# Down projection pairs one slot further behind the units whose rows they use

## The chip, the cores and the metric

The kernel runs on one core of one Trainium2 chip. The metric is the device time of one execution in microseconds, as the median of several runs. A core has five engines with instruction lists of their own, which meet through semaphores: TensorE (PE in the profile, its weight loads PEld), VectorE (DVE), ScalarE (ACT), GpSimd (POOL) and SyncE (SP), which here issues the loads of weights. TensorE writes its sums to PSUM, which has eight banks of 128 x 512 values; VectorE and ScalarE read them from there.

## The reference

Two layers over 256 positions of width 2048. Layer one mixes with a gated short convolution, layer two with latent attention; after each stands an MLP with squared ReLU, and after each part a layer norm of the scaled residual plus the part. The change lies in the MLPs alone:

```
def sq_relu_mlp(x, w1, w2):
    return jnp.square(jax.nn.relu(x @ w1)) @ w2

h = layer_norm(ALPHA * h + sq_relu_mlp(h, mlp_w1[layer], mlp_w2[layer]),
               ln_g[layer, 1], ln_b[layer, 1])
```

`w1` is 2048 x 8192 and `w2` 8192 x 2048, all in float32.

## The kernel before

**Numbers.** Every float32 operand is split in a high and a low part of TensorE's own format: `split` (lines 134 to 137) makes the high part with a copy on ScalarE and the low part with a subtraction on VectorE. A product then takes three terms: high by high, high by low, low by high. Weights arrive as `raw` tiles of 128 x 1024 in a ring of 7, and their parts `hi` and `lo` lie in rings of 9. `take` (line 192) hands out the next weights of the stream and prepares those that come after, up to a fixed distance ahead.

**Passes, units, slots.** The 8192 hidden columns are worked in 8 passes q of 8 units m. A *unit* makes 128 hidden columns for 256 positions: 16 steps of two matmuls, a high one of 512 columns (line 224) and a low one of 256 (line 228), into one PSUM bank. `whole` (line 363) adds the two halves of the bank: ScalarE copies one to SBUF (line 366), VectorE adds (line 367) into the tile `fp`, which holds two units; there is one buffer for `fp`. ReLU and square follow on ScalarE (line 732) once both units are there; the last two units of a pass of the fast kind are treated singly ("late"), the second on VectorE (line 728).

Pass 0 and pass 7 use the plain down projection (`down`). Passes 1 to 6 use a scheme with seven products instead of eight for 2 x 2 blocks. For each two units, `finish_pair` (line 650) makes sums of row blocks on VectorE (`form`, lines 645 to 648) and splits the 896 columns into *rows* `factors` (`h1c`, `h1a` in layer one, `h3c`, `h3a` in layer two; c holds rows 0 and 1, a rows 2 and 3). A *pair* (p, i) of the down projection, `products_of` and `fast_products`, multiplies the rows of units 2j and 2j+1 of pass p, j = i mod 4, with seven combinations of weight blocks: 21 matmuls of 512 columns (lines 309, 311, 312), in seven PSUM banks. Its weights (`w2f`) need more work than those of a unit: one combination on VectorE at line 171, two of half size at lines 175 and 178, and four splits (lines 136, 137). Pairs 0 to 3 serve one half of the output columns, pairs 4 to 7 the other, with the same four rows. Behind pair 3, ScalarE copies the seven banks out (line 620) and the other half's in (line 693), a burst of 14 copies. After pass 6, `fold` adds the products together, eight additions for each half (line 628).

**Order.** `steps` (line 89) gives the order of units and pairs. A *slot* is a unit and, behind it, a pair:

```
for q in range(1, NQ):
    for m in range(QC):
        p, i = (q, m - SHIFT) if m >= SHIFT else (q - 1, m + QC - SHIFT)
        yield q, m, (p, i // NB, i % NB, (p % 2) ^ (i // NB)) if p in FAST else None
```

(There, the second entry is the half and the third is j; with i as used here, pair (p, i) stands SHIFT slots behind unit (p, i).) With SHIFT = 5, pair (1,0) stands in slot (1,5), pair (1,3) in slot (2,0), pair (1,4) in slot (2,1). Units (1,0) to (1,4) and (7,5) to (7,7) have no pair: they are *lone*. A lone unit of even m uses the bank of product 6, the others the bank "unit". The rows of a pass overwrite those of the pass before, and the old rows 0 are last read by pair 4, in slot m = 1: so `finish_pair(0, u)` is called behind that slot's pair, and the other rows at m = 3, 5 and 7 as soon as their two units are done.

The written order is not quite the order on the engines: when the program is made, each engine's list is ordered by which instructions could go, and an instruction whose buffer is still taken lets later ones pass.

`mm_run` (line 230) makes a unit; at step 2 (`TURNED`) of units for which `TURN` is true the low matmul stands before the high one. In layer two (`extra`) the transposed residual is added to the sums behind units 0 to 3 of pass 1. At the end of layer one the residual is read back from memory (line 763, `xback`) into the place that the folded sums leave, and at the end of layer two `last_sum` copies the sums to PSUM, where the plain down projection goes on.

Of the kernel before, what the change touches and what calls it, by code (L numbers as in the profile page):

```python
# [18 lines left out]
T = 256  # L19
D = 2048  # L20
NC = D // P
FF = 4 * D
NQ = 8
QC = FF // NQ // P
# [10 lines left out]
NB = 4  # L35
BW = D // NB
FAST = range(1, NQ - 1)
SHIFT = 5


def TURN(q, m, extra):
    return m == 0 or not (q == 1 and m < SHIFT or q == NQ - 1 and m > SHIFT) or extra and q == 1 and m <= NB
FIRST = (0, 1, 2, 3, 4, 6, 8, 12, 16)
LEAD = 4
HEAD = 4
# [2 lines left out]
TURNED = 2  # L48
# [8 lines left out]
def trunk(ctx: ExitStack, tc: tile.TileContext, xT, vecs, lead, w_first, w_in, w_out, w_kv, w_q, w_uk, w_uv,  # L57
# [31 lines left out]
    def steps():  # L89
# [5 lines that stand above are left out]
# [15 lines left out]
    class Banks:  # L110
# [15 lines left out]
        @classmethod  # L126
        def next(cls):
            cls.count += 1
            return (cls.count - 1) % (4 if cls.more is None else 8)
# [4 lines left out]
    def split(hi, lo, src):  # L134

        nc.scalar.copy(hi, src)  # L136
        nc.vector.tensor_tensor(lo, src, hi.bitcast(F32), ALU.subtract)  # L137
# [54 lines left out]
    def take(halves=2, look=LOOK):  # L192

        i = state["next"]
        state["next"] += halves
        ahead = -sum(size(j) for j in range(i, i + halves))
        for j in range(i, len(stream)):
            for step in range(size(j)):
                ahead += 1
                if ahead > look:  # L200
                    return [ready.pop(i + k) for k in range(halves)]
                if j < 2 * HEAD:
                    continue
                steps = begun.setdefault(j, [prepare(j), 0])
                if steps[1] == step:
                    next(steps[0])
                    steps[1] += 1
        return [ready.pop(i + k) for k in range(halves)]

    def psum(name, bank=None):  # L210

        bank = Banks.next() if bank is None else bank
        return (pmm if bank < 4 else Banks.more).tile([P, 512], F32, tag=f"mm{bank}", name=name)
# [8 lines left out]
    def high(ps, w, blk, x, first):  # L222

        nc.tensor.matmul(ps, w[blk // 8][0][:, blk % 8, :], x, start=first, stop=False)  # L224

    def low(ps, w, blk, x, last):

        nc.tensor.matmul(ps[:, :T], w[blk // 8][1][:, blk % 8, :], x[:, :T], start=False, stop=last)  # L228

    def mm_run(wps, x, k0, k1, nk, turned=None):  # L230

        for k, (w, ps) in [(k, u) for k in range(k0, k1) for u in wps]:
            if k == turned:
                low(ps, w, k, x[k], False)
            high(ps, w, k, x[k], k == 0)
            if k != turned:
                low(ps, w, k, x[k], k == nk - 1)
# [125 lines left out]
    def whole(ps, out):  # L363

        t = tmp.tile([P, T], F32, tag="evac", name="t")
        nc.scalar.copy(t, ps[:, T:])  # L366
        nc.vector.tensor_tensor(out, ps[:, :T], t, ALU.add)  # L367
# [157 lines left out]
    xhl = [t[:, k, :] for t in xts for k in range(NC // 2)]  # L525
# [17 lines left out]
    for k0, k1 in pieces:  # L543
        half, at = k0 // 8, slice(k0 % 8, (k1 - 1) % 8 + 1)
        xt = xts[half][:, at, :]
        x, w = sources[k0]
# [12 lines left out]
    for m in range(NC):  # L559
        part = []  # L560
        for what in "cub":
            ps = next(pss)
            f = cbuf[:, m % 2, "cub".index(what), :T]
# [22 lines left out]
    def mlp(idx, ln, blocks, fast, begin=None, extra=None, last=False):  # L586
# [5 lines left out]
        xhl = [xt[:, k, :] for k in range(NC)]  # L592
# [40 lines left out]
        def last_sum(n, t, bank):  # L633

            finals[n, t] = psum("ps_e", bank)
            nc.scalar.copy(finals[n, t], block(n, t))
# [4 lines left out]
        def form(u):  # L641

            a21, a11, a12, s1, s2, s4 = (u[:, i * P:(i + 1) * P] for i in (0, 1, 3, 4, 6, 7))
            two = u.rearrange("p (i c) -> p i c", c=P)
            nc.vector.tensor_tensor(s1, a21, u[:, 2 * P:3 * P], ALU.add)
            nc.vector.tensor_tensor(two[:, 5:7, :], two[:, 0:5:4, :], a11.unsqueeze(1).to_broadcast([P, 2, P]),
                                    ALU.subtract)
            nc.vector.tensor_tensor(s4, a12, s2, ALU.subtract)

        def finish_pair(j, u):  # L650
            f = factors[j // 2][:, j % 2]
            if q in FAST:
                form(u)
                split(f[:, 0, :], f[:, 1, :], u[:, P:])
            else:
                split(f[:, 0, :2 * T], f[:, 1, :2 * T], u[:, :2 * T])

        q = 0
        for m in range(QC):
# [11 lines left out]
            f = tmp.tile([P, T], F32, tag="fh", name="fh", bufs=3)  # L671
# [10 lines left out]
        factors = [act.tile([P, QC // 4, 2, 7 * P], F32R, tag=tag, name=f"h{idx}{tag}") for tag in ("c", "a2")]  # L682
# [3 lines left out]
        def resume(p, g, at=None):  # L686

            ps[p] = psum(f"ps_{p}", bank[at or p])
            onto.discard(p)
            if p in OWN and begun[g] == FAST[0]:  # L690
                fresh.add(p)
            else:
                nc.scalar.copy(ps[p], place(p, g))
                onto.add(p)

        begun = {0: FAST[0], 1: FAST[0]}

        def products_of(p, i, j, g):

            nonlocal folds  # L700
            order = [f[0] for f in FACTORS]
            end = i == 0 or p == FAST[-1]
            fast_products(ps, factors, j, set(fresh), order if j == NB - 1 and end else (), onto)
            fresh.clear()
            if j == NB - 1 and end:
                begun[g] = 0
                for o in order:
                    put_back(o, g, ps[o])
                    if i == 0:
                        resume(o, 1 - g)  # L710
            if p == FAST[-1] and j == NB - 1:
                folds = chain(folds, fold(g))

        for q, m, pair in steps():
            lone = pair is None
            if q == FAST[0] and m == SHIFT:
                for o, _, _ in FACTORS:
                    resume(o, 1)
            w = take(2, 7)
            at = "6" if lone and m % 2 == 0 else "unit"  # L720
            un = psum("ps_u", bank[at])
            mm_run([(w, un)], xhl, 0, NC, NC, turned=TURNED if TURN(q, m, extra) else None)
            if m % 2 == 0:
                u = fast.tile([P, 8 * P], F32, tag="fp", name="fp")
            whole(un, u[:, (m % 2) * T:(m % 2 + 1) * T])
            late = q in FAST and m >= QC - 2
            if late and m % 2:
                nc.vector.scalar_tensor_tensor(u[:, T:2 * T], u[:, T:2 * T], 0.0, u[:, T:2 * T], ALU.max, ALU.mult)
            elif late or m % 2:
                for function in (AF.Relu, AF.Square):  # L730
                    at = u[:, :T] if late else u[:, :2 * T]
                    nc.scalar.activation(at, at, function)  # L732
            if m % 2 and (m > 1 or lone):
                finish_pair(m // 2, u)
            if extra and q == FAST[0] and m < NB:
                for t in range(2):
                    extra(block, m, t, spare[1 + (2 * m + t) % 3])
            if begin and q == FAST[0] and m < 4:
                if m % 2 == 0:
                    nc.gpsimd.dma_start(parked[:, 4 * m:4 * m + 8, :], held_x[0][:, 4 * m:4 * m + 8, :])  # L740
            if q == FAST[0] and m == SHIFT:
                sums = act.tile([P, 4, 2, BW], F32, tag="xres", name=f"sums{idx}")
            if q == NQ - 1:
                for _ in range(3 if m >= SHIFT else 2):
                    next(folds, None)
            if pair:
                products_of(*pair)
            if m == 1 and not lone:
                finish_pair(0, u)
            if q == NQ - 1 and last and m >= QC - 2:  # L750
                for t in range(2):
                    last_sum(m - QC + 2, t, spare[2 * (m - QC + 2) + t])
# [41 lines left out]
    with tc.tile_pool(name="fast1", bufs=1) as fast:  # L794
        mlp(1, before, to_wide, fast, begin=prepare_chunks)


    with tc.tile_pool(name="att", bufs=1) as ap:
# [64 lines left out]
        f = tmp.tile([P, T], F32, tag="fh", name="fpe", bufs=3)  # L863
# [223 lines left out]
    with tc.tile_pool(name="fast2", bufs=1) as fast:  # L1087
        mlp(3, after, to_out, fast, extra=turn_residual, last=True)
# [95 lines left out]
```

## Time and profile before

| | |
|---|---|
| median of 3 runs | 2000.79 us (1999.85 to 2004.03) |
| profiled execution | 2002.59 us, of it span 2000.7 us |
| granted clock of TensorE, mean | 0.998 |
| busy TensorE, VectorE, ScalarE | 1988.5, 1720.3, 1289.0 us |
| read from memory | 383.87 MB, 194 GB/s over the span |
| units and pairs, layer one | from 452.78 to 1001.80 us |
| units and pairs, layer two | from 1400.35 to 1947.56 us |

The profile shows one execution. Busy time of an engine is counted per instruction; "idle before" names what ended an idle stretch. A row of a timeline has start, duration, engine, line of the kernel, operation, what it writes and from what it reads, with shapes, and in brackets the idle time before it and what released it. The duration of a matmul includes its way through the array; the distance of the starts of two is what it costs in a stream.

### The profile page before, as it was taken

The numbers are of one execution on the slowest core, as the hardware profiler recorded it, in microseconds if no ns is written. First come the engines' busy times: TensorE is split into PE (matmuls) and PEld (weight loads), VectorE is DVE, ScalarE is ACT, GpSimd is POOL, SyncE is SP. The second block draws the span as 40 slices with busy tenths as digits, with TensorE's granted clock in tenths as the row PEclk, the third lists the DMA queues.
The fourth block names the chain that finished last, engine by engine and source line by source line (L and its number), as shares of the span: only waits on it lengthen the run. The fifth ranks groups of instructions, "written<-read, shape, count | busy, mean of one in ns | idle before, by whom it ended". The sixth has DMA issues, their size and how long they took to land.

```text
span 2000.7 us, 29698 instructions
## 1 busy us (share of the span) xinstructions
PE 1988.5 (99%) x11062; PEld 1732.5 (87%) x11062; DVE 1720.3 (86%) x2505; ACT 1289.0 (64%) x1914; POOL 5.6 (0%) x27
## 2 busy tenths in 40 slices
PE   9999999999999999999999999999999999999998
PEld 8888888988788888888889998898888888888886
DVE  8667667787899999999988988778889999999995
ACT  6444445586667777677756665558666776767772
POOL 0000000000000000000000000000000000000000
PEclk9999999999999999999999999999999999999999
DMA  9766666574565555665764643656456556565572
GB/s 339 213 190 189 189 189 190 182 238 143 180 215 191 200 194 196 210 205 204 246 223 153 184 144 106 211 182 196 140 194 216 170 203 216 180 212 197 205 267 96
DMA packets 107712, 390.00 MB, mean 195 GB/s; under 512 B 11952, under 2 KB 12720, under 8 KB 107056
## 3 DMA queue, kind: packets, MB, share of 16 engines
q1 hardware_dynamic: 106560, 383.79, 58.7%
q0 software_dynamic: 864, 4.19, 0.6%
q8 instruction: 86, 1.41, 0.3%
q14 instruction: 58, 0.48, 0.1%
q10 hardware_dynamic: 144, 0.13, 0.0%
HBM read 383.87 MB, written 4.19 MB: 194 GB/s over the span
## 4 chain that ended last, share of the span: by engine, by line
PE 95%; DMA 2%; DVE 1%; issue 1%; ACT 0%; SPq 0%; DVEq 0%; POOLq 0%; ACTq 0%
PE ps_u L224 20%; PE ps_l L224 13%; PE ps_u L228 10%; PE ps L312 7%; PE ps L311 7%; PE ps L309 7%; PE ps_l L228 7%; PE ps_d L312 2%; PE ps_d L309 2%; PE ps_d L311 2%; PE ps_w L258 2%; PE ps_w L257 2%; PE ps_w L256 2%; DMA raw<-in_w2f_dram 1%; PE ps_g L258 1%; PE ps_g L256 1%
## 5 line engine op out<-in xcount | busy, mean ns | idle before, releaser
L137 DVE TENSOR_TENSOR lo<-raw,hi 128x1024 fp32r<-128x1024 f32 x710 | 854.6, 1218 | 167.1 <-ACT hi L136 97.6
L136 ACT CAST hi<-raw 128x1024 fp32r<-128x1024 f32 x710 | 732.5, 1054 | 220.2 <-PE ps_l L224 102.2
L224 PE MATMUL ps_u<-xhl,hi 128*128 128x512 f32 x1792 | 621.2, 393 | 0.0
L228 PE MATMUL ps_u<-xhl,lo 128*128 128x256 f32 x1792 | 485.0, 280 | 0.0
L224 PEld LDWEIGHTS ps_u<-xhl,hi 128*128 128x128 f32 x1792 | 328.8, 187 | 67.5 <-DVE fp L367 0.9
L228 PEld LDWEIGHTS ps_u<-xhl,lo 128*128 128x128 f32 x1792 | 338.1, 189 | 12.9
L224 PE MATMUL ps_l<-xhl_a,hi 128*128 128x512 f32 x704 | 244.1, 393 | 0.0
L228 PE MATMUL ps_l<-xhl_a,lo 128*128 128x256 f32 x704 | 195.4, 279 | 0.0
L136 ACT CAST hi_t<-raw_t 128x1024 fp32r<-128x1024 f32 x96 | 101.5, 1057 | 120.4 <-DVE raw_t L171 115.4
L224 PEld LDWEIGHTS ps_l<-xhl_a,hi 128*128 128x128 f32 x704 | 132.1, 188 | 29.9
L228 PEld LDWEIGHTS ps_l<-xhl_a,lo 128*128 128x128 f32 x704 | 131.9, 188 | 0.2
L171 DVE TENSOR_TENSOR raw_t<-raw,raw 128x1024 f32<-128x1024 f32 x96 | 116.9, 1217 | 9.8 <-DMA raw<-in_w2f_dram 9.8
L137 DVE TENSOR_TENSOR lo_t<-raw_t,hi_t 128x1024 fp32r<-128x1024 f32 x96 | 116.9, 1218 | 2.1 <-ACT hi_t L136 1.7
L366 ACT COPY t<-ps_u 128x256 f32<-128x256 f32 x112 | 41.7, 372 | 95.0 <-PE ps_u L228 94.7
L224 PE MATMUL ps_l<-z,hi 128*128 128x512 f32 x240 | 82.4, 391 | 0.0
L258 PE MATMUL ps_w<-xd,hi 128*128 128x258 f32 x256 | 72.7, 284 | 0.0
L256 PE MATMUL ps_w<-xd,hi 128*128 128x258 f32 x256 | 72.3, 282 | 0.0
L257 PE MATMUL ps_w<-xd,lo 128*128 128x258 f32 x256 | 72.3, 282 | 0.0
L224 PE MATMUL ps_l<-oT,hi 128*128 128x512 f32 x208 | 71.3, 391 | 0.0
L732 ACT ACTIVATE fp<-fp 128x512 f32<-128x512 f32 (+1 forms) x112 | 65.9, 588 | 7.2 <-DVE fp L367 6.8
L178 DVE TENSOR_TENSOR raw<-raw 128x512 f32<-128x512 f32 x96 | 66.1, 688 | 2.0
L175 DVE TENSOR_TENSOR raw<-raw,raw_t 128x512 f32<-128x512 f32 x96 | 65.6, 683 | 0.8
(350 smaller groups left out, 3880.0 us busy)
## 6 DMA issues: line engine op xcount, KB each, us to landing
raw<-in_w_dram SPq DMA_DIRECT2D x320, 512.0 KB, 4.1
raw<-in_w2f_dram SPq DMA_DIRECT2D x192, 512.0 KB, 5.2
raw<-in_w_in_dram SPq DMA_DIRECT2D x88, 512.0 KB, 3.7
raw<-in_w_out_dram SPq DMA_DIRECT2D x32, 512.0 KB, 3.7
raw<-in_w_o_dram SPq DMA_DIRECT2D x32, 512.0 KB, 4.2
raw<-in_w_kv_dram SPq DMA_DIRECT2D x10, 512.0 KB, 4.6
raw<-in_w_q_dram SPq DMA_DIRECT2D x8, 512.0 KB, 4.0
raw<-in_w_uk_dram SPq DMA_DIRECT2D x8, 512.0 KB, 4.6
```

The source lines that it names most:

```text
L136: nc.scalar.copy(hi, src)
L137: nc.vector.tensor_tensor(lo, src, hi.bitcast(F32), ALU.subtract)
L171: nc.vector.tensor_tensor(t.rearrange(two, a=2), b12.unsqueeze(1).to_broadcast([P, 2, BW]), r1.rearrange(two, a=2), ALU.subtract)
L178: nc.vector.tensor_tensor(t4, b21, b12, ALU.subtract)
L224: nc.tensor.matmul(ps, w[blk // 8][0][:, blk % 8, :], x, start=first, stop=False)
L228: nc.tensor.matmul(ps[:, :T], w[blk // 8][1][:, blk % 8, :], x[:, :T], start=False, stop=last)
L256: nc.tensor.matmul(ps[:, :W], hi, x[k][:, :W], start=k == 0, stop=False)
L257: nc.tensor.matmul(ps[:, :W], lo, x[k][:, :W], start=False, stop=False)
L258: nc.tensor.matmul(ps[:, :W], hi, x[k][:, W:], start=False, stop=k == NC - 1)
L309: nc.tensor.matmul(ps, x[0], w[0], start=first, stop=False, skip_group_check=onto)
L311: nc.tensor.matmul(ps[:, at], x[0], w[1][:, at], start=False, stop=False, skip_group_check=onto)
L312: nc.tensor.matmul(ps, x[1], w[0], start=False, stop=last, skip_group_check=onto)
```

## The change

SHIFT goes from 5 to 6. Pair (q, i) now stands six slots behind unit (q, i): pair (1,0) in slot (1,6), pair (1,3) in slot (2,1), pair (1,4) in slot (2,2), pair (1,5) in slot (2,3). Lone units are now (1,0) to (1,5) and (7,6), (7,7). Old rows 0 and 1 are read until slots m = 2 and 3, so the new rows 0 and 1 are finished behind the pairs of those slots; a table `rows` keeps their `fp` tile until then. The parts of units 6 and 7 of pass 7 are squared and split one by one, like the late units of the other passes, instead of as two together. The bank of a lone unit goes by the distance to SHIFT, and `TURN` no longer asks whether the residual is added in (`extra`).

```
-SHIFT = 5
-def TURN(q, m, extra):
-    return m == 0 or not (q == 1 and m < SHIFT or q == NQ - 1 and m > SHIFT) or extra and q == 1 and m <= NB
+SHIFT = 6
+def TURN(q, m):
+    return m == 0 or not (q == 1 and m < SHIFT or q == NQ - 1 and m > SHIFT)
...
+        rows = {}
...
-            at = "6" if lone and m % 2 == 0 else "unit"
+            at = "6" if lone and (m - SHIFT) % 2 else "unit"
             un = psum("ps_u", bank[at])
-            mm_run([(w, un)], xhl, 0, NC, NC, turned=TURNED if TURN(q, m, extra) else None)
+            mm_run([(w, un)], xhl, 0, NC, NC, turned=TURNED if TURN(q, m) else None)
             if m % 2 == 0:
                 u = fast.tile([P, 8 * P], F32, tag="fp", name="fp")
             whole(un, u[:, (m % 2) * T:(m % 2 + 1) * T])
-            late = q in FAST and m >= QC - 2
+            late = m >= QC - 2
...
-            if m % 2 and (m > 1 or lone):
-                finish_pair(m // 2, u)
+            if late and q not in FAST:
+                f, at = factors[m // 4][:, 1], slice(m % 2 * T, (m % 2 + 1) * T)
+                split(f[:, 0, at], f[:, 1, at], u[:, at])
+            else:
+                rows[m // 2] = u
+            if m % 2 and (m > 3 or lone) and m // 2 in rows:
+                finish_pair(m // 2, rows.pop(m // 2))
...
             if pair:
                 products_of(*pair)
-            if m == 1 and not lone:
-                finish_pair(0, u)
+            if m in (2, 3) and not lone:
+                finish_pair(m - 2, rows.pop(m - 2))
```

## The prediction

> **What bounds the kernel now.** I read the page first (span, chain, busy engines), then the waits of TensorE, then the time of single units and pairs in windows, and last the timelines around the few waits.
>
> ```profile
> span 2000.7 us, 29698 instructions
> PE 1988.5 (99%) x11062; PEld 1732.5 (87%) x11062; DVE 1720.3 (86%) x2505; ACT 1289.0 (64%) x1914; POOL 5.6 (0%) x27
> PE 95%; DMA 2%; DVE 1%; issue 1%; ACT 0%; SPq 0%; DVEq 0%; POOLq 0%; ACTq 0%
> ```
>
> TensorE is busy for 99% of the span and holds 95% of the chain. The change leaves its work as it is: the same 112 units and 96 pairs. So a gain can come only from TensorE's waits, and these are short:
>
> ```profile
> PE ps L312 <- DVE h1a L137: 2.2, 1, 2.2
> PE ps_d L312 <- DVE h1a L137: 1.2, 1, 1.2
> PE ps L312 <- DVE h3a L137: 1.1, 1, 1.1
> PE ps L309 <- ACT h1a L136: 0.7, 1, 0.7
> ```
>
> All four (engine and line, what it waited for: total, times, longest) are for rows `h1a` or `h3a`, the factors made from units 4 to 7. The windows below give what each cost. Columns: stretch, its length, busy time of PE, PEld, DVE, ACT and POOL with counts, granted clock, DMA share, GB/s. Edges are the first matmuls of the unit or pair and of the one after it.
>
> ```profile
> 458.34:463.89 5.55, 5.55 (x34) 4.89 (x33) 3.04 (x4) 2.38 (x3) 0.00 (x0) 1.00 0.84 266
> 501.57:507.14 5.57, 5.57 (x34) 4.89 (x33) 4.35 (x5) 2.75 (x4) 0.00 (x0) 1.00 0.86 274
> 507.14:511.94 4.80, 4.80 (x23) 3.85 (x22) 4.04 (x6) 3.91 (x5) 0.00 (x0) 1.00 0.06 17
> 511.94:518.48 6.54, 5.81 (x33) 4.80 (x32) 6.07 (x9) 1.55 (x3) 0.00 (x0) 1.00 0.87 308
> 518.48:528.53 10.05, 7.87 (x22) 5.91 (x23) 6.03 (x7) 6.67 (x11) 0.00 (x0) 0.66 0.45 147
> 650.00:900.00 250.00, 250.00 (x1278) 212.77 (x1277) 238.48 (x290) 179.73 (x246) 0.00 (x0) 1.00 0.59 200
> 953.94:955.30 1.36, 1.36 (x7) 1.00 (x6) 1.36 (x3) 1.36 (x3) 0.00 (x0) 1.00 0.79 259
> 955.30:960.98 5.68, 5.68 (x33) 4.94 (x33) 5.68 (x7) 4.01 (x7) 0.00 (x0) 1.00 0.57 168
> 960.98:964.41 3.43, 3.43 (x17) 2.83 (x16) 3.43 (x6) 1.60 (x3) 0.00 (x0) 1.00 0.86 288
> 1006.60:1012.87 6.27, 5.07 (x22) 3.87 (x21) 3.13 (x5) 2.79 (x4) 1.06 (x2) 1.00 0.96 348
> 1406.71:1412.36 5.65, 5.65 (x36) 4.98 (x35) 3.82 (x5) 1.66 (x3) 0.00 (x0) 1.00 0.80 252
> 1468.39:1474.57 6.18, 5.09 (x23) 3.86 (x22) 5.25 (x7) 4.32 (x9) 0.00 (x0) 1.00 0.50 139
> ```
>
> A normal unit takes 5.57 us and a normal pair 4.80, so a slot 10.37 (rows 2 and 3). Rows 4 and 5 are unit (2,0) and pair (1,3) of the first layer: 0.97 and 5.25 too long, 6.22 together. The last row is pair (1,3) of the second layer, 1.38 too long. Row 6, the steady state, has TensorE busy throughout, and VectorE for 95.4%: it is nearly a second bound.
>
> **The change part by part.** The sum is made against the profiled execution: its span of 2000.7 us, 2002.59 with what lies around it. That is 1.80 above the median of 2000.79, so I take the difference over to the median.
>
> *Rows one slot earlier against their pair.* Pair (q,3) needs unit (q,7). It stood one slot behind it (unit, pair, unit, then this pair), now two, 10.37 us more. The waiting looks like this on TensorE and VectorE:
>
> ```profile
> 518.48 0.50 PE L309 MATMUL ps<-hi,h1a 128*128 128x512 f32 x1 [0.73 <-ACT h1a L136]
> 521.39 0.79 PE L312 MATMUL ps<-hi,h1a 128*128 128x512 f32 x1 [2.18 <-DVE h1a L137]
> 523.69 0.63 PE L311 MATMUL ps<-lo_t,h1a 128*128 128x512 f32 x1
> 524.12 0.63 PE L312 MATMUL ps<-hi_t,h1a 128*128 128x512 f32 x1
> ```
>
> ```profile
> 512.84 0.42 DVE L728 SCALAR_TENSOR_TENSOR fp<-fp 128x256 f32<-128x256 f32 x1
> 517.12 0.28 DVE L648 TENSOR_TENSOR fp<-fp 128x128 f32<-128x128 f32 x1
> 519.11 1.22 DVE L171 TENSOR_TENSOR raw_t<-raw,raw 128x1024 f32<-128x1024 f32 x1 [1.10 <-DMA raw<-in_w2f_dram]
> 520.26 1.08 DVE L137 TENSOR_TENSOR h1a<-fp,h1a 128x896 fp32r<-128x896 f32 x1
> 522.73 0.68 DVE L137 TENSOR_TENSOR t<-raw,t 128x512 fp32r<-128x512 f32 x1
> ```
>
> The low half of the rows stood on VectorE behind a weight step that waited for its DMA, and was done at 521.34. After the 2.18 us of idleness the matmuls start 0.43 apart (523.69 to 524.12) at a granted clock of 0.66, where 4.80/21 = 0.23 is normal; 13 or so at 0.20 more is the other 2.7 of the loss. With the new distance the rows would be done about 8 us before the pair wants them. Late next is the pair's own last weight, the split at 522.73, done at 523.41: the last three of 21 matmuls, 0.69, would end at 524.1 instead of 528.53, a gain of 4.4 if nothing else moves. But 2.5 us of row work (0.42 for the squaring at 512.84; for the sums 0.28 twice and one 128x256 operation, taken as 0.42 too; 1.08 for the split) leave this stretch of VectorE as well, so 6.2 is the other end. That the DMA wait recurs and holds the weights as long as the rows were held makes the lower end 0. I take 5.2 in layer one. In layer two the same is 1.38; I take 1.3.
>
> *Pairs 4 and 5 read the old rows later.* Rows 0 and 1 of a new pass may only be written when pairs 4 and 5 of the old pass are done. That was: rows 0 split behind the pair of m = 1. Now: behind the pair of m = 2, and rows 1 behind that of m = 3. But the buffer `fp` for units 2 and 3 is the same one that holds units 0 and 1 (one buffer). So the addition that empties unit 2's PSUM bank (line 367) now waits for the split of rows 0, which waits for pair 4, and unit 3 wants that one bank. This is a new wait, once in each of q = 2 to 7, 12 times in all. Queued behind the addition are VectorE's next weight splits; who waits is unit 3 on TensorE. Its size comes from the same place of the steady state, pair 4 of pass 2 from 617.26, here with the old order:
>
> ```profile
> 616.26 1.23 DVE L137 TENSOR_TENSOR lo<-raw,hi 128x1024 fp32r<-128x1024 f32 x1 [4.27 <-ACT hi L136]
> 623.42 0.68 DVE L137 TENSOR_TENSOR t<-raw,t 128x512 fp32r<-128x512 f32 x1
> 626.86 1.09 DVE L137 TENSOR_TENSOR h1c<-fp,h1c 128x896 fp32r<-128x896 f32 x1
> 629.01 0.42 DVE L367 TENSOR_TENSOR fp<-ps_u,t 128x256 f32<-128x256 f32 x1
> ```
>
> ```profile
> 625.88 0.95 ACT L136 CAST h1c<-fp 128x896 fp32r<-128x896 f32 x1 [1.62 <-DVE fp L648]
> ```
>
> ```profile
> 621.83 0.39 PE L312 MATMUL ps<-t,h1c 128*128 128x512 f32 x1
> 627.62 0.39 PE L309 MATMUL ps<-hi,h1c 128*128 128x512 f32 x1
> ```
>
> Pair 4 ends at 621.83+0.23 = 622.06. At the shortest the new chain is 0.95+1.09+0.42 = 2.46 us after it. If split and addition stay as far behind pair 4 as they stand here, it is 629.43-622.06 = 7.37. What covers it is pair 5: its last weight is split at 623.42, done 624.10, 3.5 us before its first matmul at 627.62, so its 21 matmuls (4.80 us) can go ahead of unit 3. That the order of TensorE does bend in this way is in rows 7 to 9 of the windows: six matmuls of pair (6,5), then unit (7,2), then the other 15, with no wait and the unit at 5.68 instead of 5.57. So the wait costs between 0 and 7.37-4.80 = 2.57 a pass. The old 7.37 came late because unit 1 and its squares ran into ScalarE's burst of bank copies behind pair 3 (VectorE's 4.27 us idle above); now unit 1 stands a slot ahead of that burst, and the sums need not wait for pair 4. So I take the short chain, covered, and pay for two bends a pass at 0.11 each (5.68-5.57): 12 x 0.2 = 2.4 us.
>
> *One more lone unit at the start, one fewer at the end.* TensorE's sum does not change. At the start VectorE has a light slot more, which helps the first pairs. At the end pass 7's pairs end one unit later, so the last eight folding additions (L628) run against two lone units instead of three, and two of them stand behind the last unit. In layer one the reload of the residual waits for them:
>
> ```profile
> 1001.63 1.64 POOL L763 DMA_DIRECT2D xback<-parked  x3 [561.45 <-DVE acc L628]
> 1006.70 0.62 ACT L136 CAST h1a<-fp 128x512 fp32r<-128x512 f32 x1
> 1009.74 0.29 DVE L419 TENSOR_SCALAR xback<-xback 128x256 f32<-128x256 f32 x1 [5.11 <-DMA xback<-parked]
> 1011.09 0.68 DVE L137 TENSOR_TENSOR h1a<-fp,h1a 128x512 fp32r<-128x512 f32 x1
> 1011.82 0.50 PE L312 MATMUL ps_d<-hi,h1a 128*128 128x512 f32 x1 [1.20 <-DVE h1a L137]
> ```
>
> The last rows were cast by 1007.32 but split only at 1011.09, behind an operation that waited 5.11 us for that DMA; TensorE lost 6.27-4.80 = 1.47. The change makes them in two halves, unit 6's a unit earlier and unit 7's with a squaring on VectorE (0.42) instead of two ScalarE passes, so the split can stand ahead of the DMA's wait: a gain up to 1.5. A reload that starts later by the two additions and the put-backs of the last pair, up to 5.6 (a unit), may cost that unit less the 3.1 us between 1009.74 and 1012.87, behind which the first matmul stands that needs it: 2.5. I take a gain of 0.7.
>
> *The order of two products in a unit (TURN).* In layer two units 1 to 4 of pass 1 lose the reversed order. With it a unit took 5.65 (1406.71), the plain lone unit of layer one 5.55 (458.34); four times 0.10 is 0.4 at best. The transposes between them speak against the whole of it, so I take 0.2, with 0.2 of loss as the other end. The swap of the two banks of lone units is without cost: banks still alternate, with a unit of 5.55 us to empty each.
>
> Sum: -5.2 -1.3 +2.4 -0.7 -0.2 = -5.0 us. That is 2002.59 to 1997.6 for the profiled execution and 2000.79 to 1995.8 in the median.
>
> **The rivals.** *The wait for unit 2's bank is not covered.* If splits and addition keep their 7.37 us behind pair 4, TensorE idles 2.57 us in each of 12 passes: 30.8 instead of 2.4, and 2000.79-7.4+30.8 = 2024. VectorE's 95.4% and the late 626.86 speak for it; the bends of rows 7 to 9, where nothing idles, against. It decides from (7.4)/12 = 0.6 us a pass. If every such wait also slowed the clock as at 518.48, 2.7 more each, it would be 2056.
>
> Here the Trainium skill bears, "TensorE: Matmul & The Clock Gate", Part 1: the clock falls to half after an idle window of about 3.4 us that runs freely, and a cold matmul of 512 columns starts every 426.7 ns. The trace agrees on the 0.43 us, but fell after waits of 0.73 and 2.18 us with two matmuls between. By the rule only some of the 12 waits would be followed by slow matmuls, so between the two times.
>
> *VectorE is the real bound.* Its gaps in the steady state are those of the burst alone, so the 6 us that TensorE stops losing at the start come back as waits for weights later: no change, 2000. Against it: layer two, with only 1.38 us lost at its start, shows no later wait of TensorE in its passes.
>
> *The start's waits stay,* since the DMA of the weights makes them: 2000.79+2.4-0.9 = 2002.
>
> *The end of layer one gets 2.5 longer:* 1995.8+0.7+2.5 = 1999.
>
> **How the numbers follow.** Forecast 0.48; wait uncovered in whole or part 0.26 (2001 to 2024, mostly the lower half); VectorE 0.10; start's waits stay 0.10; end longer 0.06. A measurement of this kernel tells about 0.2%, 4.0 us. The forecast's own range is 1991.3 (terms at their best: -6.2-1.4+0-1.5-0.4 = -9.5) to 1999. The whole range is 1991 to 2011: about 0.12 lies above it, upper parts of the uncovered wait, and 0.04 below. Faster by over 0.2% (below 1996.8) 0.45: most of the forecast's case; within 0.2% 0.28; slower 0.27.
>
> **What would show it.** Right: no wait of TensorE for `h1a` or `h3a` in pass 1 or 2, granted clock 1.00 there, pair (1,3) at 4.80; in each later pass the first matmuls of pair 5 ahead of unit 3, and no wait of `ps_u` for `fp` L367. Wrong: waits of `ps_u` for `fp` L367 of 0.6 us or more once a pass; a wait for `lo` L137 or `hi` at the first pairs; `xback` landing later than 1013 with a wait behind it.

## The result and the profile after

The changed kernel takes 2009.57 us (median of 5, 2008.62 to 2011.01); the kernel before, in the same comparison, 2000.43 us. The ratio is 1.0044, with a 95% interval of 1.0029 to 1.0058: slower by 0.44%, where 0.25% faster was forecast. The profiled execution took 2011.01 us.

The head of its page, and four of its six rows of waits of TensorE (engine and line, what it waited for: total, times, longest; the other two lie outside the units and pairs):

```profile
span 2007.7 us, 29706 instructions
PE 1991.5 (99%) x11062; PEld 1729.0 (86%) x11062; DVE 1727.2 (86%) x2509; ACT 1284.0 (64%) x1916; POOL 5.6 (0%) x27
PE 82%; DVE 8%; ACT 7%; issue 2%; DVEq 0%; ACTq 0%
```

```profile
PE ps_u L224 <- DVE fp L367: 4.0, 4, 1.2
PE ps L309 <- ACT hi L136: 2.5, 6, 0.5
PE ps L309 <- ACT t L136: 1.7, 4, 0.5
PE ps L311 <- DVE t L137: 1.0, 2, 0.5
```

The old waits for rows (`h1a`, `h3a`) are gone. In their place stand waits of units for `fp` (unit 3 waits until unit 2's bank is emptied), and of pairs for their own weights, `hi` and `t`. VectorE and ScalarE now hold 15% of the chain, where TensorE had 95% alone.

The passes say where the time went. The table has the time in us from the first matmul of a pass's first unit to that of the next pass, and behind pass 7 to the first matmul of the plain down projection. The change takes one pair (4.80) out of pass 1 and puts one into pass 7.

| | 1 | 2 | 3 | 4 | 5 | 6 | 7 |
|---|---|---|---|---|---|---|---|
| before, layer one | 59.16 | 89.20 | 83.11 | 82.93 | 82.99 | 83.03 | 68.59 |
| after, layer one | 54.31 | 84.43 | 83.04 | 83.96 | 84.71 | 84.75 | 75.58 |
| before, layer two | 62.47 | 84.31 | 82.95 | 82.94 | 82.97 | 83.03 | 68.53 |
| after, layer two | 57.90 | 84.07 | 83.04 | 84.17 | 84.70 | 84.75 | 75.58 |

Eight undisturbed slots of 10.37 us are 82.96. The start of layer one has lost its 6 us of waiting for rows, but pass 2 still takes 1.5 and 1.1 us more than 82.96, and from pass 4 on a loss sets in that grows to 1.7 us a pass, and 2.2 in pass 7 (75.58-4.80 = 70.78 against 68.59 and 68.53).

Windows of the changed kernel (stretch, length, busy PE, PEld, DVE, ACT, POOL with counts, granted clock, DMA share, GB/s): unit (2,1) and pair (1,3) of layer one; around pair 4 and pair 5 in pass 3; the same in pass 5; pass 5 as a whole.

```profile
517.16:522.72 5.56, 5.56 (x33) 4.89 (x32) 3.32 (x5) 2.14 (x3) 0.00 (x0) 1.00 0.63 203
522.72:527.52 4.80, 4.80 (x23) 3.95 (x22) 4.80 (x6) 3.33 (x6) 0.00 (x0) 1.00 0.35 82
617.51:622.32 4.81, 4.81 (x24) 3.95 (x22) 4.57 (x5) 4.81 (x7) 0.00 (x0) 1.00 0.38 112
622.32:625.95 3.63, 3.63 (x18) 2.88 (x16) 3.63 (x6) 2.62 (x4) 0.00 (x0) 1.00 0.58 173
625.95:631.55 5.60, 5.60 (x33) 4.93 (x33) 5.53 (x6) 2.34 (x3) 0.00 (x0) 1.00 0.80 266
784.29:789.09 4.80, 4.80 (x23) 3.94 (x22) 1.62 (x2) 4.80 (x8) 0.00 (x0) 1.00 0.22 90
789.09:795.50 6.41, 5.51 (x23) 3.54 (x21) 6.41 (x8) 5.66 (x8) 0.00 (x0) 1.00 0.45 166
795.50:796.07 0.57, 0.57 (x3) 0.47 (x3) 0.57 (x2) 0.00 (x0) 0.00 (x0) 1.00 0.96 180
758.22:842.92 84.70, 83.80 (x425) 70.37 (x424) 80.40 (x98) 59.98 (x83) 0.00 (x0) 1.00 0.58 199
```

Rows 1 and 2: unit and pair at the start are at their normal time, at full clock. Rows 3 to 5, pass 3: behind pair 4, 16 matmuls of pair 5 go ahead of unit 3 in 3.63 us, without a gap. Rows 6 to 8, pass 5: now all 21 of pair 5 and two of pair 6 go ahead, and they take 6.41+0.57 = 6.98 us instead of 23 x 4.80/21 = 5.26. The loss of 1.72 is nearly the whole loss of the pass. What they wait for, on TensorE, VectorE and ScalarE of the changed kernel:

```profile
793.02 0.39 PE L312 MATMUL ps<-hi,h1c 128*128 128x512 f32 x1
793.86 0.49 PE L309 MATMUL ps<-t,h1c 128*128 128x512 f32 x1 [0.45 <-ACT t L136]
794.80 0.73 PE L309 MATMUL ps<-hi,h1a 128*128 128x512 f32 x2 [0.45 <-ACT hi L136]
796.07 0.40 PE L224 MATMUL ps_u<-xhl,hi 128*128 128x512 f32 x1
```

```profile
787.47 2.36 DVE L137 TENSOR_TENSOR lo<-raw,hi 128x1024 fp32r<-128x1024 f32 x2 [3.22 <-ACT hi L136]
792.62 1.22 DVE L137 TENSOR_TENSOR lo<-raw,hi 128x1024 fp32r<-128x1024 f32 x1
793.75 1.09 DVE L137 TENSOR_TENSOR h1c<-fp,h1c 128x896 fp32r<-128x896 f32 x1
794.75 0.69 DVE L137 TENSOR_TENSOR t<-raw,t 128x512 fp32r<-128x512 f32 x1
795.35 0.42 DVE L367 TENSOR_TENSOR fp<-ps_u,t 128x256 f32<-128x256 f32 x1
```

```profile
789.46 2.04 ACT L136 CAST hi<-raw 128x1024 fp32r<-128x1024 f32 x2
791.36 0.98 ACT L136 CAST h1c<-fp 128x896 fp32r<-128x896 f32 x1
793.15 0.66 ACT L136 CAST t<-raw 128x512 fp32r<-128x512 f32 x1
```

Unit 3 starts at 796.07, right behind the addition at 795.35 that empties unit 2's bank into `fp` and is done at 795.77, 6.68 us behind pair 4's end; and that stands behind the split of rows 0 (cast at 791.36, subtraction at 793.75), which could not begin before pair 4's end at 789.09. Until then TensorE eats up pair 5, faster than its last weights `t` come: cast at 793.15, low half done at 795.44. Both the bank and the weights are late, and both stand in the one list of VectorE, which has no gap from 787.47 on.

### The profile page after: what moved, and what is told of

The parts are those of the page before. It is cut to its first block, busy times and chain, and to the rows that moved or that the text cites. A ratio compares the mean times of both kernels' runs of the same rounds, so it can differ in the third digit from the quotient of the medians.

```text
span 2007.7 us, 29706 instructions
## 1 busy us (share of the span) xinstructions
PE 1991.5 (99%) x11062; PEld 1729.0 (86%) x11062; DVE 1727.2 (86%) x2509; ACT 1284.0 (64%) x1916; POOL 5.6 (0%) x27
## 4 chain that ended last, share of the span: by engine, by line
PE 82%; DVE 8%; ACT 7%; issue 2%; DVEq 0%; ACTq 0%
PE ps_u L224 16%; PE ps_l L224 13%; PE ps_u L228 8%; PE ps_l L228 7%; PE ps L311 5%; PE ps L312 4%; PE ps L309 4%; DVE lo L137 3%; ACT hi L136 3%; PE ps_d L309 2%; PE ps_d L311 2%; PE ps_d L312 2%; PE ps_w L258 2%; PE ps_w L257 2%; PE ps_w L256 2%
```

## The experiments

Two theories stood at first. A: the loss is the wait for the one buffer `fp`, which keeps unit 2's bank full until pair 4 is done. B: it is the crowd of work on ScalarE and VectorE behind pair 3, brought next to pairs 4 and 5 by the shift, whether there is one buffer or two.

**Unit 2 emptied into a tile of its own.** `fp` keeps its one buffer; unit 2 goes into a 128 x 256 tile of a ring that is idle in these passes.

```
+            aside = m in (2, 3) and not lone
+            if m == 2 and aside:
+                first = tmp.tile([P, T], F32, tag="fh", name="first", bufs=3)
+            elif m % 2 == 0 or aside:
                 u = fast.tile([P, 8 * P], F32, tag="fp", name="fp")
-            whole(un, u[:, (m % 2) * T:(m % 2 + 1) * T])
+            whole(un, first if m == 2 and aside else u[:, (m % 2) * T:(m % 2 + 1) * T])
...
+            elif aside and m == 3:
+                nc.scalar.activation(u[:, :T], first, AF.Relu)
+                nc.scalar.activation(u[:, T:2 * T], u[:, T:2 * T], AF.Relu)
+                nc.scalar.activation(u[:, :2 * T], u[:, :2 * T], AF.Square)
...
-            else:
+            elif m != 2 or not aside:
                 rows[m // 2] = u
```

> The changed kernel, but unit 2 of passes 2 to 7 is emptied into a small tile of its own (128 x 256), so that its PSUM bank no longer waits for the buffer fp that pair 4 holds; its ReLU then goes from that tile into fp, one ScalarE operation more a pass. Theory A (the loss is this wait, 8.1 us a layer from pass 2 on): passes of 84.7 us fall back to about 83.0, TensorE no longer waits for the weights of pair 5, the gain at the start stays: 1994 to 1997 us. Theory B (the loss is the crowd on ScalarE and VectorE behind pair 3, which the shift brings next to pairs 4 and 5, and would be there without the buffer): passes stay near 84.7, 2007 to 2010 us.

Measured: 1998.96 us, ratio to the kernel before 0.9986 (0.9978 to 0.9995). Passes 2 to 6 of layer two take 82.93, 82.94, 83.15, 83.21 and 83.19, pass 7 takes 73.36 (68.56 without the pair). These are passes 2 and 5 of layer one, and then the three longest waits of TensorE:

```profile
507.18:590.11 82.93, 82.93 (x426) 70.67 (x424) 76.79 (x95) 57.94 (x79) 0.00 (x0) 1.00 0.56 190
756.60:839.83 83.23, 83.23 (x426) 70.44 (x424) 79.10 (x97) 59.85 (x83) 0.00 (x0) 1.00 0.59 202
```

```profile
PE mu0p L421 <- DVE xback L419: 2.5, 1, 2.5
PE ps_e L1084 <- ACT umeans L1082: 1.6, 1, 1.6
PE warm L383 <- DVE col L384: 1.1, 1, 1.1
```

TensorE is busy throughout both passes. Theory A holds and B falls: of 84.7 us, 83.2 are left. Units 3 and 5, which take up to 0.14 more than the normal 5.57 in layer one, hold a part of the rest over 82.96; TensorE does not wait. The median is 2 us above what A expected, and the waits show why: a new one of 2.5 us for the residual `xback` at the end of layer one.

**The parts of pass 7 alone**, on the kernel before:

```
-            late = q in FAST and m >= QC - 2
+            late = m >= QC - 2
...
+            if late and q not in FAST:
+                f, at = factors[m // 4][:, 1], slice(m % 2 * T, (m % 2 + 1) * T)
+                split(f[:, 0, at], f[:, 1, at], u[:, at])
-            if m % 2 and (m > 1 or lone):
+            elif m % 2 and (m > 1 or lone):
                 finish_pair(m // 2, u)
```

> The kernel before, with one part of the change alone: units 6 and 7 of pass 7 are squared and split one by one. Theory A and B: the stall of 1.47 us at the end of layer one goes or stays, nothing else moves: 1998.5 to 2000.8 us. If the parts were what cost time in pass 7, it is 2002 or more.

Measured: 1999.63 us, 0.9988 (0.9979 to 0.9997). From the first matmul of the plain down projection of layer one to the mean of the residual it takes 10.93 us, where the kernel before takes 12.45: the stall of 1.5 us goes.

**The change without the parts**, the reverse:

```
-            late = m >= QC - 2
+            late = q in FAST and m >= QC - 2
```

> The changed kernel without the one-by-one parts of pass 7 (units 6 and 7 squared and split together, as before). Theory A: passes 2 to 6 as in the changed kernel, the end of layer one 1.5 us longer or the same: 2009.5 to 2011.5 us. If the parts cost time: below 2008.

Measured: 2009.88 us, 1.0044 (1.0032 to 1.0057), as with them. The stretch at the end of layer one takes 10.93 us here too. So beside the shift the parts are worth nothing. VectorE splits the last rows here (1007.66 to 1008.34) ahead of the operation that waits for the residual (1009.12), where the kernel before had them behind it; why that order turned was not tested.

**The old rule of reversed order**, in the changed kernel:

```
+    return m == 0 or not (...) or extra and q == 1 and m <= NB
```

> The changed kernel with the old rule of reversed order in layer two (units 1 to 4 of pass 1 reversed, behind the transposes). Units 1 to 4 there took 5.64, 5.74, 5.63 and 5.63 us without it and 5.65 with it: no difference over 0.3 us, 2009.3 to 2010 us, under either theory.

Measured: 2009.67 us, 1.0046 (1.0034 to 1.0059): no difference.

**Four folding additions at each lone unit.** This goes after the 2.5 us that the first experiment left over; it keeps that experiment's edit.

```
-                for _ in range(3 if m >= SHIFT else 2):
+                for _ in range(4 if m >= SHIFT else 2):
                     next(folds, None)
```

> The first experiment's kernel (unit 2 emptied into a tile of its own), with four folding additions taken at each of the two lone units of pass 7 instead of three, so that none is left behind them. There TensorE waited 2.65 us for the residual read back in layer one and ran at a lower granted clock after it (a block 1.8 us longer). If that wait comes from the reload that starts behind the last folding addition, the reload starts some 1.9 us sooner, and 2 to 4 us go: 1995 to 1997 us. If the wait has another cause: 1998 to 2000.

Measured: 1995.39 us, 0.9973 (0.9962 to 0.9984): it beats the kernel before clear of the noise. In the first experiment, GpSimd's row of the reload, the operation of VectorE that wants its first part, and windows of the last six matmuls before the wait and of the block of 21 behind it:

```profile
1002.30 1.64 POOL L776 DMA_DIRECT2D xback<-parked  x3 [0.25 <-DVE acc L628]
1009.65 0.29 DVE L419 TENSOR_SCALAR xback<-xback 128x256 f32<-128x256 f32 x1 [4.25 <-DMA xback<-parked]
```

```profile
1006.00:1010.00 4.00, 1.52 (x7) 0.94 (x5) 0.35 (x2) 1.04 (x1) 0.13 (x1) 1.00 1.02 396
1010.35:1016.93 6.58, 6.58 (x24) 5.24 (x22) 6.51 (x13) 1.43 (x2) 0.05 (x1) 0.74 0.97 366
```

The same in this experiment:

```profile
1001.65 1.64 POOL L776 DMA_DIRECT2D xback<-parked  x3 [561.67 <-ACT h1a L136]
1006.25 0.29 DVE L419 TENSOR_SCALAR xback<-xback 128x256 f32<-128x256 f32 x1 [1.29 <-DMA xback<-parked]
```

```profile
1006.68:1008.05 1.37, 1.37 (x8) 1.13 (x7) 1.37 (x2) 0.00 (x0) 0.85 (x2) 1.00 1.04 425
1008.29:1013.29 5.00, 5.00 (x24) 4.11 (x22) 5.00 (x11) 2.33 (x3) 0.00 (x0) 1.00 1.03 417
```

The plain down projection begins at 996.43 there and at 997.12 here. So the reload starts 5.87 us behind that point there and 4.53 here, and 4.00 falls to 1.37 and the block behind it from 6.58 to 5.00. The operation on VectorE comes 13.22 us behind that point there and 9.13 here. The earlier start is 1.34 of these 4.09; the rest is a quicker reload, 7.35 us there and 4.60 here from its start to that operation. Why it was quicker was not tested.

**VectorE made lighter.** Theory A says that there is a wait; it does not say why pair 5 fails to cover it. Two half-size combinations of each pair's weights were left out, in the changed kernel and in the one before; the products are then not the right ones, and VectorE has 1.4 us less to do in each slot.

```
-        nc.vector.tensor_tensor(b12, b22, t[:, :BW], ALU.subtract)
...
-        nc.vector.tensor_tensor(t4, b21, b12, ALU.subtract)
```

> The changed kernel with the two half-size combinations of each pair's weights (lines 175 and 178, 0.69 us each on VectorE) left out, so that the products are not the right ones; VectorE has 1.4 us less in each slot of 10.37. Theory C (pair 5 cannot cover unit 2's wait because VectorE has its last weights only just in time): passes fall from 84.7 to at most 0.3 us over those of the light kernel before, 83.2 or less. Theory D (the wait itself is longer than pair 5): passes stay 1.0 us or more above them.

> The kernel before with the same two combinations left out: passes of 82.9 to 83.0 us, since TensorE is the bound already; the start of layer one without most of its 6.2 us if VectorE's lag made the rows late, with them if the DMA wait did.

Measured: 1996.05 us for the light changed kernel, 1994.81 for the light kernel before. Pass 5 of layer one, first of the light changed kernel, then of the light kernel before:

```profile
756.43:839.55 83.12, 83.12 (x426) 70.58 (x424) 71.04 (x82) 61.34 (x82) 0.00 (x0) 1.00 0.62 203
```

```profile
760.91:843.89 82.98, 82.98 (x425) 70.58 (x424) 70.98 (x82) 61.58 (x82) 0.00 (x0) 1.00 0.62 203
```

VectorE is busy for 71 us of the pass instead of 80, and the loss falls from 1.72 to 0.14, though all of pair 5 and two matmuls of pair 6 still go ahead of unit 3 there, in 4.76+0.52 us. So it is VectorE's load that leaves the wait uncovered. The time falls as theory C said, but this run does not part C from D, since it makes the wait shorter too. Two rows of VectorE in the light changed kernel, where pair 4 ends at 787.53:

```profile
787.23 0.68 DVE L137 TENSOR_TENSOR t<-raw,t 128x512 fp32r<-128x512 f32 x1
792.24 0.42 DVE L365 TENSOR_TENSOR fp<-ps_u,t 128x256 f32<-128x256 f32 x1
```

Pair 5's last weight is done at 787.91, and unit 2's bank is empty at 792.66, 5.13 us behind pair 4's end. In the changed kernel that is 6.68, and the 23 matmuls that go ahead cover 5.26 of it: the bank alone would have kept at least 1.42 of the 1.72 with every weight in time. The light kernel before also loses most of its start: pass 2 of layer one takes 83.87 us instead of 89.20, with 0.6 us of waiting for `h1a` left. The size of that start varies between executions: the kernel with the parts alone, the same as the kernel before up to pass 7, has 87.55 there. Even so, the fall to 83.87 is larger than that, so the rows were late because VectorE was, more than because of the DMA before them.

## Why the prediction was wrong, step by step

*Rows one slot earlier: right.* Taken at 5.2 and 1.3, the waits of 6.27 (89.20 to the 82.93 of the first experiment) and 1.38 (84.31 to 82.93) went whole (in the fifth experiment, the same kernel up to pass 7, pass 2 of layer one took 83.67, so the first can be 0.7 less). Pair (1,3) takes 4.80 at full clock. The row of the pair's own last weights, as next late, did not bind.

*Pairs 4 and 5 read the old rows later: the step that failed.* The wait, its place and the order of TensorE around it were as described. What failed is "I take the short chain, covered". The chain from pair 4's end to unit 2's empty bank was taken at 2.46 us, and its price at 0.2 us a pass, 2.4 in all. In passes 2 to 7 it took 5.10, 3.45, 5.66, 6.68, 6.68 and 7.48 us in layer one, and 4.73, 3.45, 5.93, 6.68, 6.68 and 7.48 in layer two: only in pass 3 is it well below the 4.80 of pair 5. The reason for the short chain was that unit 1 now stands ahead of ScalarE's burst. It does, but the casts and splits of weights that pile up behind the burst stand ahead of rows 0 on both engines: in pass 5 the cast of rows 0 starts 2.27 us and their split 4.66 us behind pair 4's end.

Against 82.93 for a full pass, and 73.39 and 73.33 for pass 7 with the pair added, passes 2 to 7 lose 1.50, 0.11, 1.03, 1.78, 1.82 and 2.19 in layer one and 1.14, 0.11, 1.24, 1.77, 1.82 and 2.25 in layer two: 16.8 us.

The working sized wait and cover at one place, pair 4 from 617.26, one pass behind the stall of layer one, and used it for all twelve. At that place the new kernel loses what was worked out: 16 matmuls go ahead without a gap, the bank is empty 3.45 us behind pair 4's end at 622.32, and 0.11 is lost.

```profile
625.35 0.42 DVE L367 TENSOR_TENSOR fp<-ps_u,t 128x256 f32<-128x256 f32 x1
```

But it was the kindest place. In pass 5 the kernel before shows, with pair 4 from 783.12 to 787.92:

```profile
783.12:787.92 4.80, 4.80 (x23) 3.95 (x22) 2.65 (x3) 4.80 (x8) 0.00 (x0) 1.00 0.32 88
```

```profile
785.27 2.36 DVE L137 TENSOR_TENSOR lo<-raw,hi 128x1024 fp32r<-128x1024 f32 x2 [3.43 <-ACT hi L136]
791.89 0.69 DVE L137 TENSOR_TENSOR t<-raw,t 128x512 fp32r<-128x512 f32 x1
796.65 1.09 DVE L137 TENSOR_TENSOR h1c<-fp,h1c 128x896 fp32r<-128x896 f32 x1
```

Pair 5's last weight is done at 792.58, 4.66 us behind pair 4's end, where pass 3 had 2.04. Pair 5 needs it for the last three of its 21 matmuls, 18 x 0.23 = 4.1 us after it begins. So the cover was already short by half a microsecond in the trace that was there. The split of rows 0 was later too: done 9.82 us behind pair 4's end, where pass 3 had 5.89. In the changed kernel the last weight is done 6.35 us behind it (795.44-789.09), of which 1.09 is the split of rows 0, which now stands ahead of the weight on VectorE. The late weights are one half of the failure; in pass 2 they have no part, as the rows of VectorE and TensorE show:

```profile
539.84 0.69 DVE L137 TENSOR_TENSOR t<-raw,t 128x512 fp32r<-128x512 f32 x1
542.58 0.42 DVE L367 TENSOR_TENSOR fp<-ps_u,t 128x256 f32<-128x256 f32 x1
```

```profile
543.14 0.47 PE L224 MATMUL ps_u<-xhl,hi 128*128 128x512 f32 x1 [1.24 <-DVE fp L367]
```

There the last weight is ready at 540.53, 17 matmuls of pair 5 go ahead, and unit 3 waits 1.24 us for the bank alone. That the wait for the bank is the loss is shown by the first experiment, and that VectorE's load leaves it uncovered by the light kernels; where both are late, as in pass 5, the rows leave at most 0.3 (1.72-1.42) to the weights alone, but no run tested that, nor why the lag settles after pass 4.

*The end of layer one: inside its bounds, but by luck.* A gain of 0.7 between +1.5 and -2.5 was taken; 1.5 came, but the change has it without the parts too, which were the reason given. The late reload, named as the loss, did not cost the changed kernel anything; it cost the first experiment 2.65 us and a slow block, where TensorE arrived earlier.

*TURN: no difference,* within the bounds given (2009.67 against 2009.57).

*The rivals.* The first one, the uncovered wait, is what happened, in the lower half of its stretch, at 1.4 us a pass against the 0.6 from which it decides. Its two supports were VectorE's 95.4% and the late 626.86; they deserved more than 0.26. "VectorE is the real bound" was half right: not for the start's gain, which stayed, but for the cover. The slow clock did not follow these waits: the passes run at a granted clock of 1.00.

The sum of the terms as measured, -6.3-1.4+16.8-1.5, is 7.6 us; the span grew by 7.0. The rest to the 9.1 us between the medians lies around the span (2011.01-2007.7 = 3.3 us in the profiled execution after, 1.9 in the one before) and in how far each profiled execution stands above its median.

## What to carry to other kernels

A wait that other work is to cover has two sizes to look up, in every pass and not in one: how long the wait lasts, and when the last input of the cover is ready. This matters above all where one engine that is busy for 95% makes both. When a step is moved past another, ask which single buffer it now holds longer, and who is emptied into that buffer; here a tile of 128 x 256 in an idle ring turned 9 us of loss into a gain of 0.14%. When a stall goes, look at what stood behind it: the reload of the residual became a stall only once TensorE came earlier.

## What the runs showed of the hardware

After a single wait of 2.5 us in the first experiment TensorE's granted clock fell to 0.74 over the next block of 21 matmuls, which took 6.58 us instead of 5.00, while in the units and pairs of the changed kernel waits of 1.24 us and less left it at 1.00. The window behind the longest of these:

```profile
543.14:549.00 5.86, 5.86 (x33) 5.17 (x34) 5.79 (x7) 4.44 (x6) 0.00 (x0) 1.00 0.47 165
```

The Trainium skill, "TensorE: Matmul & The Clock Gate", Part 1, puts the idle window at about 3.4 us; here 2.5 was enough, and where the window lay is not in the trace.
